# A two-layer decoder step: fewer VectorE instructions, a mask constant of another form, the samples stored with the last quarter, and side products at other places of the matmul stream

## The chip, the cores and the metric

The kernel runs on one core of one Trainium2 chip. The metric is the device time of one execution in microseconds. Three executions of the kernel before took 597.88, 597.41 and 596.48 us, a median of 597.41.

The engines are named as in the profile: PE is TensorE (matrix products, and transposes by a product with the identity), DVE is VectorE, ACT is ScalarE, POOL is GpSimd, and SP is SyncE, which here mostly issues transfers. Each engine works through its own list of instructions in order. An instruction waits on semaphores that other engines or transfers raise.

## The reference, cut to what matters

One step of a decoder with two layers, for a prompt of 256 positions and eight samples of one position each, with 256 earlier positions in a paged cache. All arithmetic is float32.

```python
# layer 0
h = rmsnorm(x, norm_g);  z = h @ w_in                    # q, k, v, bu, bv
a = moba_attention(rope(q), rope(k), v)                  # softmax, causal
bvn = layer_norm(gelu(bv), sgu_gain)
b_out = gelu(bu) * (tril(sgu_w) @ bvn + sgu_b)           # chunks of 128
x = x + concat(a, b_out) @ w_out
x = conv_ffn(x)                                          # x + (gelu(conv3(h @ w_gate)) * (h @ w_up)) @ w_down
# layer 1
q, k, v, u = split(rmsnorm(x) @ w_in)
c = stick_breaking_attention(q, k, v)
pooled = mean of the last w rows of u, w = 2, 4, 8, 16 by group of 128 channels; at position i < w the mean is over i + 1 rows
d = ((pooled - u) @ pool_w) * pool_scale
x = x + concat(c, d) @ w_out
x = conv_ffn(x)
y = rmsnorm(x, final_norm)                               # y_prompt, y_sample
```

The outputs are y for the prompt and the samples, the new keys and values of both layers, the normalised bv rows of the samples, and the new pooling and convolution states.

## The kernel before

**Layout.** Activations lie transposed: 128 channels on the partitions, 264 columns (256 prompt positions, then 8 samples). X holds the residual as eight such slices. Attention probabilities are the other way round, with queries on the partitions, so they are transposed on PE before they meet the values.

**Matrix products.** Each weight block of 128 x 128 is split into a rounded part `wh` (ACT, line 299) and the rest `wl` (DVE, line 302), and each activation likewise into `_h` and `_l`. One block then is three matmuls of 264 columns: wh with h, wh with l, wl with h. A weight tile has eight blocks, and its split is written three tiles ahead of its use (`split`, LOOK = 3). The function `run` goes through a phase's blocks in a fixed order, in0, out0, ff0, dn0, in1, out1, ff1, dn1, with 160, 64, 352, 176, 128, 64, 352 and 176 blocks; `evac` moves a finished accumulator out of PSUM.

**Side work at block numbers.** Everything beside these products is hooked on a block count: `blk(b, f)` calls f once b blocks of the phase are written. Within in0 (bv, q, k, bu, v, 32 blocks each) these are for each pair of heads the scores (`s_qk`) with the softmax behind them (`s_soft`), the transposes of one head's probabilities (`s_tr`), the mean and the squares of the gated branch (`gm_mean`, `gm_var`, `gm_norm`; PE products pmu and ns_sgu), its transposes (`gm_tr`, vtp_sgu) and the gating products (`gm_gate`, pf), the sample scores (`sm_score`, `sm_soft`) and the transposes of the values (`v_pair`, vtp_v). Within in1 (u, q, k, v) they are the pooling sums (`pool_sum`), one pooling product per group (`pool_mix`, pm), the stick-breaking scores (`z_qk`, `stick`), their transposes (`z_tr`, pt), the sample scores (`zs_score`) and again `v_pair`.

**What sets the order.** `keep_in_program_order` fixes the transfers, PE from in0 on, and some single instructions. The others on DVE, ACT and POOL are put in order by a scheduler when the program is built, so that an edit can exchange neighbours on those engines. Accumulators and side products on PE share PSUM banks in rotation: four for the tag mm, four for the tag at.

**Places the change touches.**
- Constants: ones, epst and onesr (lines 385 to 390), made on DVE; the causal mask m0 among the loaded constants, copied twice into mask0 by `masks` (line 760); `sgu_load` (lines 880 to 885) builds a lower triangle tril of zeros and ones out of m0 and the identity on DVE and multiplies the gating weights by it on POOL.
- `zs_score` puts the sample queries into qz (line 474) and `zs_out` the sample results into osam (line 1119) with DVE copies.
- `pool_sum` (line 1139 on) makes, for each of four windows, a doubled sum, the scaled difference pl, and two small instructions hd and pl (lines 1143 and 1144) that correct the first w positions, where the mean is over fewer rows.
- `final` (from line 626): X, scaled by the gain, is transposed back in sixteen pieces `turn(b, m)` into four PSUM banks yt, while row sums of squares give R for the two prompt halves (ns_row) and Rs for the samples (ns_col). DVE and ACT scale the banks into Y, and five stores go out, three on SP and two on ACT.

Of the kernel before, what the change touches and what calls it, by code (L numbers as in the profile page):

```python
# [9 lines left out]
F32 = mybir.dt.float32  # L10
# [8 lines left out]
P = 128  # L19
# [130 lines left out]
def _consts():  # L150
    f = np.float32
    parts = []

    def add(name, a):
        full = np.zeros((P, a.shape[1]), f)
        full[: a.shape[0]] = a
        _CST[name] = (sum(x.shape[1] for x in parts), a.shape[1])
        parts.append(full)

    half = 8  # L160
    inv = (f(500000.0) ** (-(np.arange(half, dtype=f) * f(2.0) / f(16)))).astype(f)
    pos = np.concatenate([np.arange(SEQ), np.full(NS, PAST)]).astype(f)
    ang = (pos[None, :] * inv[:, None]).astype(f)
    c, s = np.cos(ang.astype(np.float64)).astype(f), np.sin(ang.astype(np.float64)).astype(f)
    C, S = np.ones((P, T), f), np.zeros((P, T), f)
    for b in (0, 64):
        C[b:b + 8], C[b + 8:b + 16] = c, c
        S[b:b + 8], S[b + 8:b + 16] = -s, s
    r = np.arange(P)
    global _ROPE, _EDGE  # L170

    _EDGE = np.zeros((P, 384), f)
    _EDGE[r[1:], r[1:]], _EDGE[r, 2 * P + r] = 1, 1
    _ROPE = np.ascontiguousarray(np.concatenate([C, S], 1))
    add("ident", np.eye(P, dtype=f))
    add("m0", np.where(r[None, :] > r[:, None], f(NEG), f(0)).astype(f))
    g32, h32 = r // 32, r % 32
    used = (h32 < 2 * NS)[:, None]
    ts = np.arange(4 * NS)[None, :]
    add("sm", (used & (g32[:, None] == ts // NS) & (h32[:, None] // 2 == ts % NS)).astype(f))  # L180
    add("hs", (used & (h32[:, None] % 2 == r[None, :] // HD)).astype(f))
    add("icnt", np.concatenate([np.tile((f(1) / np.minimum(np.arange(16) + 1, w).astype(f))[None, :], (P, 1)) for w in POOLW], 1))
    return np.ascontiguousarray(np.concatenate(parts, 1))
# [8 lines left out]
    ("sguw", (P, 512)), ("sgub", (P, 512)), ("poolw", (P, 512)),  # L192
]
_OUTS = [
    ("y", (2, P, D)), ("ys", (P, KD, NS)), ("k0", (P, 4, T)), ("v0", (P, 4, T)), ("bvn", (P, 4, NS)),
    ("k1", (P, 4, T)), ("v1", (P, 4, T)), ("poolp", (P, 4, NST)), ("pools", (P, 4, NS, 16)),
    ("cv0", (P, NF, 10)), ("cv1", (P, NF, 10)), ("cs0", (P, NF, NS)), ("cs1", (P, NF, NS)),
]
# [3 lines left out]
def tile_decoder_step(ctx: ExitStack, tc: tile.TileContext, a):  # L202
# [180 lines left out]

    ident = cst("ident")
    ones = con.tile([P, P], F32, name="ones")
    v.memset(ones, 1.0)
    onesr = con.tile([P, P], F32R, name="onesr")
    v.tensor_copy(onesr, ones)
    epst = con.tile([P, 1], F32, name="epst")
    v.memset(epst, EPS)  # L390


    def operand_tile(dst, m, src, gain, pin=False):
# [211 lines left out]
    def final():  # L605
# [25 lines left out]
        def rest():  # L631
            acc = nrm.acc
            p, q = [mmb(f"ns_row{b}") for b in range(2)], mmb("ns_col")
            yt = [[at(f"y{b}{h}") for h in range(2)] for b in range(2)]

            def turn(b, m):
                keep(pe.transpose(yt[b][m // 4][:, m % 4 * P:m % 4 * P + P], X[:, m, b * P:b * P + P], ident))

            def total(b, x, **k):
                keep(pe.matmul(p[b][:, 0:1], x[:, b * P:b * P + P], ones[:, 0:1], **k))  # L640

            R = [sm.tile([P, 1], F32, tag=f"Rf{b}", name=f"R_fin{b}", bufs=1) for b in range(2)]
            Rs = sm.tile([P, NS], F32, tag="Rfs", name="R_fins", bufs=1)

            def rstd(r, x):
                keep(s.activation(r, x, AF.Ln, bias=epst, scale=1.0 / D))
                keep(s.activation(r, r, AF.Exp, scale=-0.5))

            total(0, acc, start=True, stop=False)
            total(1, acc, start=True, stop=False)  # L650
            for m in range(3):
                turn(0, m)
            total(0, sq, start=False, stop=True)
            rstd(R[0], p[0][:, 0:1])
            turn(0, 3)
            total(1, sq, start=False, stop=True)
            rstd(R[1], p[1][:, 0:1])
            for m in range(4, 8):
                turn(0, m)
            keep(pe.matmul(q[:, :NS], ones, acc[:, SEQ:], start=True, stop=False))  # L660
            keep(pe.matmul(q[:, :NS], ones, sq[:, SEQ:], start=False, stop=True))
            for m in range(8):
                turn(1, m)
            Y = [f4(f"y{b}", (P, D)) for b in range(2)]
            ys = sm.tile([P, KD, NS], F32, tag="bvn", name="ys", bufs=1)

            def byv(b, c0, c1):
                keep(v.tensor_scalar(Y[b][:, c0:c1], yt[b][c0 // 512][:, c0 % 512:c0 % 512 + c1 - c0], R[b], None, ALU.mult))

            def bys(b):  # L670
                keep(s.activation(Y[b][:, 512:], yt[b][1], AF.Copy, scale=R[b]))

            def store(e, b, c0, c1):
                keep(e.dma_start(a["y"][b][:, c0:c1], Y[b][:, c0:c1]))

            byv(0, 0, 256)
            store(nc.sync, 0, 0, 256)
            byv(0, 256, 512)
            bys(0)
            store(s, 0, 256, D)  # L680
            rstd(Rs, q[:, :NS])
            byv(1, 0, 512)
            store(nc.sync, 1, 0, 512)
            bys(1)
            keep(v.tensor_tensor(ys, X[:, :, SEQ:T], Rs.unsqueeze(1).to_broadcast([P, KD, NS]), ALU.mult))
            keep(nc.sync.dma_start(a["ys"], ys))
            store(s, 1, 512, D)
        return evac, rest

    def pick(xg):  # L690
# [65 lines left out]
    g.memset(mask0, 0.0)  # L756

    def masks():
        for b in (0, SEQ):
            tc.keep_in_program_order(s.activation(mask0[:, b:b + P], cst("m0"), AF.Copy))  # L760

    q4, k4, v4 = f4("q4"), f4("k4"), f4("v4")
    bv4, bu4 = f4("bv4"), f4("bu4")
# [115 lines left out]
    def sgu_load():  # L879
        late(sguc[:, 0], a["sguw"].rearrange("p (g t) -> p g t", t=P))  # L880
        late(sguc[:, 1], a["sgub"].rearrange("p (g t) -> p g t", t=P))
        tril = sm.tile([P, T], F32, tag="acc", name="tril", bufs=2)[:, :P]
        tc.keep_in_program_order(v.tensor_scalar(tril, cst("m0"), 0.0, None, ALU.is_lt))
        v.tensor_tensor(tril, tril, ident, ALU.add)
        g.tensor_tensor(sguc[:, 0], sguc[:, 0], tril.unsqueeze(1).to_broadcast([P, 4, P]), ALU.mult)

    def sum4(e, t4, name):
        acc = sm.tile([P, T], F32, tag="acc", name=name, bufs=2)
# [82 lines left out]
    blk(64, late, VEC, a["vec"])  # L971
    blk(72, sm_q)
    for t in range(4):
        blk((94, 120)[t // 2], s_qk, t)
    for t, b in enumerate((109, 115, 133, 140)):
        blk(b, s_tr, 2 * t)
        blk(b, s_tr, 2 * t + 1)
    blk(96, sgu_load)
    blk(100, gm_mean)
    blk(119, gm_var)  # L980
    blk(120, sm_score)
    blk(120, sm_soft)
    blk(131, gm_gelu)
    blk(133, gm_norm)
    blk(149, sm_tr)
    blk(120, late, a["k0"], k4)
    blk(156, lambda: late(a["bvn"], st0["bvn"]))
    for t in range(4):
        blk((148, 148, 150, 150)[t], gm_tr, t)
    blk(152, gm_own)  # L990
    for t in range(4):
        blk((153, 153, 157, 157)[t], gm_gate, t)
    for t, b in enumerate((146, 154, 162)):
        if b <= 160:
            blk(b, lambda t=t: v_pair(vt, v4[:, t, :], t, "v0"))
# [106 lines left out]

    def zs_score():
        ps = mmb("sc1")
        sample_score(ps, sample_q(qz1, q4, v.tensor_copy), ktiles, range(NS))
        w = st1["zs"] = pp.tile([P, PAST], F32, tag="p", name="zs")
        stick_all(w, ps[:, :PAST])

# [7 lines left out]
    def zs_out():  # L1116
        osam = sm.tile([P, 4, NS], F32, tag="osam", name="osam1", bufs=1)
        for b, q, po in sample_out(st1["msk"], "l1"):
            v.tensor_copy(osam[b:b + 64, :, q:q + 4], po)
        halves(catA[0][:, :, SEQ:T], catA[1][:, :, SEQ:T], osam)  # L1120


# [10 lines left out]
    def pool_sum():  # L1133
# [3 lines left out]
        for t, W in enumerate(POOLW):  # L1137
            d = A if t % 2 == 0 else B
            v.tensor_tensor(d[:, t:, PW:], src[:, t:, PW:], src[:, t:, PW - W // 2:PW + SEQ - W // 2], ALU.add)
            src = d  # L1140
            v.scalar_tensor_tensor(pl[:, t, :SEQ], src[:, t, PW:], 1.0 / W, U[:, t, PW:], ALU.mult, ALU.subtract)
            hd = sm.tile([P, 16], F32, tag="hd", name=f"hd{t}", bufs=2)
            v.tensor_tensor(hd[:, :W], src[:, t, PW:PW + W], icnt[:, t, :W], ALU.mult)
            v.tensor_tensor(pl[:, t, :W], hd[:, :W], U[:, t, PW:PW + W], ALU.subtract)
            ss = sm.tile([P, NS], F32, tag="ss", name=f"ss{t}", bufs=2)
            v.tensor_reduce(ss, PALL[:, t, :, 16 - W:16], AX.X, ALU.add)
            v.scalar_tensor_tensor(pl[:, t, SEQ:T], ss, 1.0 / W, PALL[:, t, :, NST], ALU.mult, ALU.subtract)

    def pool_mix(t):
        pm = mmb(f"pm{t}")  # L1150
# [29 lines left out]
    blk(84, late, a["poolp"], plp)  # L1180
    blk(84, late, a["pools"], PALL)
    blk(112, late, a["k1"], k4)
    for i, b in enumerate((62, 66, 70, 76)):
        blk(b, pool_mix, i)
    for t, b in enumerate((113, 120, 126)):
        blk(b, lambda t=t: v_pair(vt, v4[:, t, :], t, "v1", mmb))
    run(orders["in1"], pick(xg), in1_evac, hk)
    hk = Hooks()
# [86 lines left out]
```

## Time and profile before

| | us |
|---|---|
| median of three executions | 597.41 |
| the profiled execution | 596.68 |
| its span, first to last instruction | 594.9 |
| PE busy | 586.5 |
| DVE busy | 421.2 |
| ACT busy | 344.5 |
| POOL busy | 108.3 |

The span is what the trace covers; the time of an execution also has what lies around it, here 1.8 us. In a list of instructions a row has the start, the duration, the engine, the line, the operation, what it writes and reads, and in brackets how long the engine was idle before it and what ended that. Matmuls overlap in their pipeline, and one that takes 0.28 us follows the last by 0.12; so PE's throughput is read from the distance of starts, or from the chain of work, which gives a run of matmuls as one piece. The waits list names the waiting instruction, what it waited for, the total in us, how often and the longest. The windows give for a stretch its length, then busy time and number of instructions on each engine, the granted PE clock, the share of the transfer engines' time and GB/s.

### The profile page before, as it was taken

To read this page: it belongs to the slowest core of one execution; us is meant where nothing else is said; L and a number is where in the kernel's file an instruction comes from. 1 tells how busy PE (TensorE), PEld (TensorE's weight loads), DVE (VectorE), ACT (ScalarE), POOL (GpSimd) and SP (SyncE) were. 2 spreads that over 40 slices of the span, in tenths; PEclk is the share of its full clock that TensorE was granted. 3 is DMA by queue.
4 is the path that set the end of the run, shared out by engine and by line. 5 is a ranking of instruction groups with operands and counts; after the bars stand their busy time and mean duration, and the time that the engine had idled before them with its cause. 6 is when DMAs were issued, how large, how long until landed. Compare 5 with 4: busy or idle time off the path is not lost.

```text
span 594.9 us, 12426 instructions
## 1 busy us (share of the span) xinstructions
PE 586.5 (99%) x4913; PEld 571.6 (96%) x4913; DVE 421.2 (71%) x754; ACT 344.5 (58%) x605; POOL 108.3 (18%) x100
## 2 busy tenths in 40 slices
PE   9999999999999999999999999999999999999996
PEld 8998989999999999999999897999999999999995
DVE  6999676878787778665659685687878787864431
ACT  7747955676555555644453475567655555564442
POOL 2100031222322222110110000122232322211110
PEclk9999999999999999999999999999999999999999
DMA  9898872545454555895568765254545555455502
GB/s 342 326 404 310 329 252 82 203 158 197 158 198 166 190 174 182 296 371 188 187 217 290 242 235 177 82 203 156 199 153 202 167 188 175 181 190 196 189 1 74
DMA packets 27708, 122.42 MB, mean 206 GB/s; under 512 B 3458, under 2 KB 4482, under 8 KB 16258
## 3 DMA queue, kind: packets, MB, share of 16 engines
q1 hardware_dynamic: 27072, 120.30, 56.8%
q10 hardware_dynamic: 578, 1.32, 0.6%
q8 instruction: 39, 0.64, 0.4%
q14 instruction: 19, 0.16, 0.1%
HBM read 117.65 MB, written 3.96 MB: 204 GB/s over the span
## 4 chain that ended last, share of the span: by engine, by line
PE 92%; DVE 5%; ACT 1%; issue 1%; DVEq 0%
PE mm L214 84%; DVE wl L302 2%; PE sc L214 1%; PE pv_l L214 1%; PE pav L214 1%; PE pt L217 1%; PE warm L214 1%; DVE keep L1062 1%; PE Z L214 0%; ACT wh L299 0%; PE y L217 0%; DVE rz_k L774 0%; PE pf L214 0%; PE pm L214 0%; PE vtp_v L217 0%
## 5 line engine op out<-in xcount | busy, mean ns | idle before, releaser
L302 DVE TENSOR_TENSOR wl<-raw,wh 128x1024 fp32r<-128x1024 f32 x179 | 218.5, 1222 | 70.0 <-ACT wh L299 64.7
L299 ACT ACTIVATE wh<-raw 128x1024 fp32r<-128x1024 f32 x179 | 188.4, 1055 | 87.5 <-PE mm L214 78.4
L214 PE MATMUL mm<-xg_f_h,wh 128*128 128x264 f32 x704 | 200.1, 284 | 0.0
L214 PE MATMUL mm<-xg_f_l,wh 128*128 128x264 f32 x704 | 199.9, 284 | 0.0
L214 PE MATMUL mm<-xg_f_h,wl 128*128 128x264 f32 x704 | 198.6, 282 | 0.0
L214 PEld LDWEIGHTS mm<-xg_f_l,wh 128*128 128x128 f32 x704 | 132.2, 188 | 0.0
L214 PEld LDWEIGHTS mm<-xg_f_h,wl 128*128 128x128 f32 x704 | 132.2, 188 | 0.0
L214 PEld LDWEIGHTS mm<-xg_f_h,wh 128*128 128x128 f32 x704 | 132.2, 188 | 0.0
L584 POOL TENSOR_TENSOR wk<-wk 128x264 f32<-128x264 f32 x44 | 66.4, 1511 | 193.9 <-DVE wk L583 173.0
L214 PE MATMUL mm<-a_h,wh 128*128 128x264 f32 x352 | 100.1, 284 | 0.0
L214 PE MATMUL mm<-a_l,wh 128*128 128x264 f32 x352 | 99.9, 284 | 0.0
L214 PE MATMUL mm<-a_h,wl 128*128 128x264 f32 x352 | 99.4, 282 | 0.0
L214 PEld LDWEIGHTS mm<-a_l,wh 128*128 128x128 f32 x352 | 66.1, 188 | 0.0
L214 PEld LDWEIGHTS mm<-a_h,wh 128*128 128x128 f32 x352 | 66.1, 188 | 0.0
L214 PEld LDWEIGHTS mm<-a_h,wl 128*128 128x128 f32 x352 | 66.1, 188 | 0.0
L444 ACT ACTIVATE a_h<-wk 128x264 fp32r<-128x264 f32 x44 | 18.7, 424 | 73.1 <-POOL wk L584 73.1
L445 DVE TENSOR_TENSOR a_l<-wk,a_h 128x264 fp32r<-128x264 f32 x44 | 19.2, 436 | 41.5 <-ACT a_h L444 41.5
L214 PE MATMUL mm<-xg_h,wh 128*128 128x264 f32 x160 | 47.5, 297 | 0.0
L214 PE MATMUL mm<-xg_l,wh 128*128 128x264 f32 x160 | 45.8, 287 | 0.0
L214 PE MATMUL mm<-xg_h,wl 128*128 128x264 f32 x160 | 45.6, 285 | 0.0
L214 PE MATMUL mm<-xg_n_h,wh 128*128 128x264 f32 x128 | 38.0, 297 | 0.0
L214 PE MATMUL mm<-xg_n_l,wh 128*128 128x264 f32 x128 | 36.3, 283 | 0.0
(260 smaller groups left out, 903.3 us busy)
## 6 DMA issues: line engine op xcount, KB each, us to landing
raw<-in_w SPq DMA_DIRECT2D x89, 1024.0 KB, 4.8
K<-in_kt SPq DMA_DIRECT2D x32, 256.0 KB, 6.8
V<-in_vp SPq DMA_DIRECT2D x32, 256.0 KB, 5.8
raw<-in_w SPq DMA_DIRECT2D x4, 512.0 KB, 5.8
X<-in_x SPq DMA_DIRECT2D x4, 264.0 KB, 6.4
xw<-in_xw SPq DMA_DIRECT2D x2, 388.0 KB, 5.4
out_k<-k SPq DMA_DIRECT2D x1, 528.0 KB
out_v<-v SPq DMA_DIRECT2D x1, 528.0 KB, 2.8
```

What stands on the lines that cost most here:

```text
L214: return self.keep(nc.tensor.matmul(*x, **k))
L217: return self.keep(nc.tensor.transpose(*x, **k))
L299: i = s.activation(h, src, AF.Copy)
L302: i = v.tensor_tensor(l, src, h.bitcast(F32), ALU.subtract)
L444: s.activation(h, src, AF.Copy)
L445: v.tensor_tensor(l, src, h.bitcast(F32), ALU.subtract)
L584: g.tensor_tensor(A, A, C, ALU.mult)
L1062: v.tensor_tensor_scan(keep[:, 1:n][:, ::-1], keep[:, 1:n][:, ::-1], edge[:, 1:][:, ::-1], 0.0, ALU.mult, ALU.max)
```

## The change

- ones and epst are set by POOL, and onesr is copied by ACT inside `masks`, instead of by DVE.
- The constant m0 (0 and -1e30) becomes low (1 where the column is not below the row, else 0). mask0 is low shifted by one column and scaled by -1e30, and the gating weights are multiplied by low directly; both tril instructions go.
- The copies into qz and osam of layer 1 move from DVE to ACT.
- The eight edge instructions of `pool_sum` become four, each for the two groups whose sums share a buffer, behind all four sums.
- The final stage: four of the second half's transposes come ahead of ns_col. The stores are regrouped into three outputs: y0 in two stores, y1 in one, all three on SP, and y2, the last quarter of the prompt together with the samples, in one store on ACT. ys is no longer a store of its own.
- Block numbers: `s_qk` and `sm_score`, `sm_soft` from 120 to 121, `s_tr` of heads 2 and 3 from 115 to 119, `gm_var` from 119 to 120, `gm_tr` from 148, 148, 150, 150 to 149, 150, 151, 152, the first two `gm_gate` from 153 to 154; in layer 1 `pool_mix` from 62, 66, 70, 76 to 68, 71, 74, 78 and `v_pair` from 113, 120, 126 to 113, 123, 127.

In the built program DVE has 733 instructions in place of 748, ACT 601 in place of 595, POOL 107 in place of 105; PE and SP have as many as before.

```diff
-    add("m0", np.where(r[None, :] > r[:, None], f(NEG), f(0)).astype(f))
+    add("low", (r[None, :] >= r[:, None]).astype(f))
...
-    v.memset(ones, 1.0)
+    g.memset(ones, 1.0)
     onesr = con.tile([P, P], F32R, name="onesr")
-    v.tensor_copy(onesr, ones)
     epst = con.tile([P, 1], F32, name="epst")
-    v.memset(epst, EPS)
+    g.memset(epst, EPS)
...
+            for m in range(4):
+                turn(1, m)
             keep(pe.matmul(q[:, :NS], ones, acc[:, SEQ:], start=True, stop=False))
             keep(pe.matmul(q[:, :NS], ones, sq[:, SEQ:], start=False, stop=True))
-            for m in range(8):
+            for m in range(4, 8):
                 turn(1, m)
...
-            byv(0, 0, 256)
-            store(nc.sync, 0, 0, 256)
-            byv(0, 256, 512)
-            bys(0)
-            store(s, 0, 256, D)
-            rstd(Rs, q[:, :NS])
-            byv(1, 0, 512)
-            store(nc.sync, 1, 0, 512)
-            bys(1)
-            keep(v.tensor_tensor(ys, X[:, :, SEQ:T], Rs.unsqueeze(1).to_broadcast([P, KD, NS]), ALU.mult))
-            keep(nc.sync.dma_start(a["ys"], ys))
-            store(s, 1, 512, D)
+            byv(Y[0][:, :256], 0, 0, 256)
+            keep(nc.sync.dma_start(a["y0"][:, :256], Y[0][:, :256]))
+            byv(Y[0][:, 256:H], 0, 256, H)
+            bys(Y[0][:, H:], 0)
+            keep(nc.sync.dma_start(a["y0"][:, 256:], Y[0][:, 256:]))
+            byv(Y[1], 1, 0, H)
+            keep(nc.sync.dma_start(a["y1"], Y[1]))
             rstd(Rs, q[:, :NS])
+            bys(Y[2][:, :H], 1)
+            keep(v.tensor_tensor(Y[2][:, H:].rearrange("p (m s) -> p m s", s=NS), X[:, :, SEQ:T], Rs.unsqueeze(1).to_broadcast([P, KD, NS]), ALU.mult))
+            keep(s.dma_start(a["y2"], Y[2]))
...
     def masks():
+        tc.keep_in_program_order(s.activation(onesr, ones, AF.Copy))
         for b in (0, SEQ):
-            tc.keep_in_program_order(s.activation(mask0[:, b:b + P], cst("m0"), AF.Copy))
+            tc.keep_in_program_order(s.activation(mask0[:, b + 1:b + P], cst("low")[:, :P - 1], AF.Copy, scale=NEG))
...
-        tril = sm.tile([P, T], F32, tag="acc", name="tril", bufs=2)[:, :P]
-        tc.keep_in_program_order(v.tensor_scalar(tril, cst("m0"), 0.0, None, ALU.is_lt))
-        v.tensor_tensor(tril, tril, ident, ALU.add)
-        g.tensor_tensor(sguc[:, 0], sguc[:, 0], tril.unsqueeze(1).to_broadcast([P, 4, P]), ALU.mult)
+        g.tensor_tensor(sguc[:, 0], sguc[:, 0], cst("low").unsqueeze(1).to_broadcast([P, 4, P]), ALU.mult)
...
-        blk((94, 120)[t // 2], s_qk, t)
-    for t, b in enumerate((109, 115, 133, 140)):
+        blk((94, 121)[t // 2], s_qk, t)
+    for t, b in enumerate((109, 119, 133, 140)):
...
-    blk(119, gm_var)
-    blk(120, sm_score)
-    blk(120, sm_soft)
+    blk(120, gm_var)
+    blk(121, sm_score)
+    blk(121, sm_soft)
...
-        blk((148, 148, 150, 150)[t], gm_tr, t)
+        blk((149, 150, 151, 152)[t], gm_tr, t)
...
-        blk((153, 153, 157, 157)[t], gm_gate, t)
+        blk((154, 154, 157, 157)[t], gm_gate, t)
...
-        sample_score(ps, sample_q(qz1, q4, v.tensor_copy), ktiles, range(NS))
+        sample_score(ps, sample_q(qz1, q4, lambda o, i: s.activation(o, i, AF.Copy)), ktiles, range(NS))
...
-            v.tensor_copy(osam[b:b + 64, :, q:q + 4], po)
+            s.activation(osam[b:b + 64, :, q:q + 4], po, AF.Copy)
...
-            hd = sm.tile([P, 16], F32, tag="hd", name=f"hd{t}", bufs=2)
-            v.tensor_tensor(hd[:, :W], src[:, t, PW:PW + W], icnt[:, t, :W], ALU.mult)
-            v.tensor_tensor(pl[:, t, :W], hd[:, :W], U[:, t, PW:PW + W], ALU.subtract)
...
+        for e, src in enumerate((A, B)):
+            hd = sm.tile([P, 2, 16], F32, tag="hd", name=f"hd{e}", bufs=2)
+            v.tensor_tensor(hd, src[:, e::2, PW:PW + 16], icnt[:, e::2, :], ALU.mult)
+            v.tensor_tensor(pl[:, e::2, :16], hd, U[:, e::2, PW:PW + 16], ALU.subtract)
...
-    for i, b in enumerate((62, 66, 70, 76)):
+    for i, b in enumerate((68, 71, 74, 78)):
         blk(b, pool_mix, i)
-    for t, b in enumerate((113, 120, 126)):
+    for t, b in enumerate((113, 123, 127)):
```

More of the change, by code (lines that the diff above doesn't have):

```diff
@@ L194 @@
 _OUTS = [
-    ("y", (2, P, D)), ("ys", (P, KD, NS)), ("k0", (P, 4, T)), ("v0", (P, 4, T)), ("bvn", (P, 4, NS)),
+    ("y0", (P, D)), ("y1", (P, D // 2)), ("y2", (P, D // 2 + KD * NS)), ("k0", (P, 4, T)), ("v0", (P, 4, T)), ("bvn", (P, 4, NS)),
     ("k1", (P, 4, T)), ("v1", (P, 4, T)), ("poolp", (P, 4, NST)), ("pools", (P, 4, NS, 16)),
@@ L659, in rest, with byv, bys @@
                 turn(0, m)
+            for m in range(4):
+                turn(1, m)
             keep(pe.matmul(q[:, :NS], ones, acc[:, SEQ:], start=True, stop=False))
             keep(pe.matmul(q[:, :NS], ones, sq[:, SEQ:], start=False, stop=True))
-            for m in range(8):
+            for m in range(4, 8):
                 turn(1, m)
[L664 to L674, printed above, removed]
-            byv(0, 0, 256)
-            store(nc.sync, 0, 0, 256)
-            byv(0, 256, 512)
-            bys(0)
-            store(s, 0, 256, D)
-            rstd(Rs, q[:, :NS])
-            byv(1, 0, 512)
-            store(nc.sync, 1, 0, 512)
-            bys(1)
-            keep(v.tensor_tensor(ys, X[:, :, SEQ:T], Rs.unsqueeze(1).to_broadcast([P, KD, NS]), ALU.mult))
-            keep(nc.sync.dma_start(a["ys"], ys))
-            store(s, 1, 512, D)
+            H = D // 2
+            Y = [f4(f"y{i}", (P, w)) for i, w in enumerate((D, H, H + KD * NS))]
+            def byv(dst, b, c0, c1):
+                keep(v.tensor_scalar(dst, yt[b][c0 // H][:, c0 % H:c0 % H + c1 - c0], R[b], None, ALU.mult))
+            def bys(dst, b):
+                keep(s.activation(dst, yt[b][1], AF.Copy, scale=R[b]))
+            byv(Y[0][:, :256], 0, 0, 256)
[5 more added lines that the diff above has]
+            keep(nc.sync.dma_start(a["y1"], Y[1]))
+            rstd(Rs, q[:, :NS])
+            bys(Y[2][:, :H], 1)
+            keep(v.tensor_tensor(Y[2][:, H:].rearrange("p (m s) -> p m s", s=NS), X[:, :, SEQ:T], Rs.unsqueeze(1).to_broadcast([P, KD, NS]), ALU.mult))
+            keep(s.dma_start(a["y2"], Y[2]))
         return evac, rest
@@ L1254 @@
     o = {n: np.asarray(r.results[0]["out_" + n]) for n, _ in _OUTS}
-    y = np.concatenate([o["y"].reshape(SEQ, D), o["ys"].transpose(2, 1, 0).reshape(NS, D)])
+    y1 = np.concatenate([o["y1"], o["y2"][:, :D // 2]], 1)
+    y = np.concatenate([o["y0"], y1, o["y2"][:, D // 2:].reshape(P, KD, NS).transpose(2, 1, 0).reshape(NS, D)])
     def kv(k, w):
```

## The prediction

> **What bounds the kernel now.** I read the page's first part, then the list of what TensorE (PE) waited for, then the busy time by stage.
>
> ```profile
> span 594.9 us, 12426 instructions
> ...
> PE 586.5 (99%) x4913; PEld 571.6 (96%) x4913; DVE 421.2 (71%) x754; ACT 344.5 (58%) x605; POOL 108.3 (18%) x100
> ```
>
> ```profile
> PE pt L217 <- DVE p L811: 1.0, 1, 1.0
> PE vtp_v L217 <- DVE v4b L1164: 0.6, 1, 0.6
> ```
>
> ```profile
> 18.73:52.35 33.62, 32.59 (x272) 31.78 (x270) 32.95 (x91) 22.99 (x43) 1.29 (x1) 1.00 0.94 363
> ...
> 350.00:375.00 25.00, 24.45 (x217) 20.65 (x217) 14.69 (x22) 15.29 (x32) 0.00 (x0) 1.00 0.53 170
> ...
> 400.18:586.50 186.32, 186.32 (x1541) 186.32 (x1541) 122.22 (x202) 101.82 (x167) 40.84 (x28) 1.00 0.46 160
> 586.50:594.90 8.40, 2.86 (x25) 2.39 (x24) 2.38 (x8) 2.98 (x10) 0.00 (x0) 0.94 0.36 130
> ```
>
> The columns are PE, PEld, DVE, ACT and POOL, then the granted clock and the DMA share. PE has no gap in the long stages and the change takes no matmul away, so only three things can get shorter: the two PE waits, each inside a stage where DVE's queue runs late (32.95 of 33.62 us busy in the first), and the last 8.4 us, where PE is nearly done and copies and stores end the kernel. A DVE instruction saved anywhere else is worth nothing.
>
> **The first wait (layer 0).** PE's own rows:
>
> ```profile
> 50.83 0.49 PE L217 MATMUL pt<-CST,p 128*128 128x128 f32 x3
> 52.35 0.55 PE L217 MATMUL pt<-CST,p 128*128 128x128 f32 x3 [1.03 <-DVE p L811]
> ```
>
> ```profile
> 52.90 1.47 PE mm L214 x12
> 54.36 0.45 PE pmu L214 x2
> ```
>
> Three transposes at 0.11 us each from 50.83 would have let the next start at 51.16; it started at 52.35, so 1.19 us is lost. The change puts these transposes (heads 2 and 3) behind block 119 instead of 115: four blocks of three matmuls, 12 x 0.122 = 1.47 us. PE then asks for the fourth head's probabilities at about 50.83 + 1.47 + 0.33 = 52.63. What is ready by then:
>
> ```profile
> 46.73 0.22 DVE L883 TENSOR_SCALAR tril<-CST 128x128 f32<-128x128 f32 x1
> ...
> 48.95 0.29 DVE L884 TENSOR_TENSOR tril<-tril,CST 128x128 f32<-128x128 f32 x1
> ...
> 49.58 1.38 DVE L890 TENSOR_TENSOR bsum<-bsum,bv 128x264 f32<-128x264 f32 x1
> ...
> 52.02 0.27 DVE L811 TENSOR_SCALAR p<-p,st 128x128 f32<-128x128 f32 x1
> 52.22 0.42 DVE L891 TENSOR_TENSOR bsum<-bsum,bv 128x264 f32<-128x264 f32 x1
> ```
>
> ```profile
> 49.38 1.29 POOL L885 TENSOR_TENSOR sguc<-sguc,tril 128x512 f32<-128x512 f32 x1 [32.78 <-DVE tril L884]
> ```
>
> The DVE normalisation ended at 52.29, so even unchanged it is ready 0.3 us ahead of PE. The two tril instructions leave the queue: from start to start they take 0.14 and 0.21 us. The second bsum addition took 1.38 us where the third took 0.42: the 0.96 us lies under the POOL multiply of 1.29 us, which now waits only for its weights, no longer for tril. Its start is bounded by 49.38 (now) and, were its transfer landed long before, by DVE's earlier two-input operations; the collision costs DVE between 0 and 1.29 us. I take the measured 0.96, so DVE is 0.35 us ahead and the margin is 0.7 us; at 1.29 it is still 0.3. The Trainium skill, "SBUF — State Buffer", section "Who interferes with whom", has DVE instructions with two SBUF inputs locked out for a whole POOL instruction that reads SBUF. By that rule the loss would be up to the full 1.29 us, and the end of the sum is the same; the trace agrees on the block (1.38 against 0.42).
>
> Head scores and their mean matmul (pmu) shift from 119/120 to 120/121, in the same order, and bsum's third addition (52.64 at the latest) is there before PE reaches pmu at about 53.3. So this wait goes whole: 1.19 us, bounds 0.9 and 1.2.
>
> **What is late next in layer 0.** ACT does not get earlier: in the new order a weight copy stands ahead of mu on ACT, the matching weight difference ahead of the subtraction on DVE, and the last head's Copy behind a table load, so its row of work up to the layer norm's scale keeps its hours. PE arrives there 1.19 us sooner.
>
> ```profile
> 70.69 0.44 ACT L434 ACTIVATE R_sgu<-R_sgu 128x264 f32<-128x264 f32 x1
> ```
>
> ```profile
> 71.96 1.70 DVE L917 SCALAR_TENSOR_TENSOR bv<-bv,VEC,R_sgu 128x264 f32<-128x264 f32 x4
> ```
>
> ```profile
> 72.67 0.27 PE vtp_sgu L217 x2
> ...
> 73.77 0.22 PE pP L217 x2
> 73.99 0.14 PE pO L214 x2
> ```
>
> Before, PE met the first vtp_sgu at 72.67. Now block 148 comes at 71.48, then a block (0.37) and pP and pO (0.36): 72.2. The first of four normalised slices is ready a quarter into 1.70 us, at 72.4. PE waits 0.2 us, and the spread over blocks 149 to 152 lets the other three pass; before, the pair at 148 lost about as much (pitch 0.25 between slices one and two). I count 0; bounds -0.2 and +0.6. The gating products stand one block later and find their slices ready.
>
> **The second wait (layer 1).**
>
> ```profile
> 357.83 0.28 PE L214 MATMUL mm<-xg_n_h,wl 128*128 128x264 f32 x1
> 358.66 0.44 PE L217 MATMUL vtp_v<-CST,v4b 128*128 128x128 f32 x2 [0.55 <-DVE v4b L1164]
> ```
>
> ```profile
> 358.20 0.41 DVE L1164 TENSOR_TENSOR v4b<-mm,R_n 128x264 f32<-128x264 f32 x1
> ...
> 360.12 0.42 DVE L1164 TENSOR_TENSOR v4b<-mm,R_n 128x264 f32<-128x264 f32 x1
> ```
>
> PE could have gone on at 357.95; 0.71 us is lost on v4b, held up by stick-breaking on DVE. Moved from 120 to 123, the transpose comes after three blocks (1.1) and six score transposes (0.66, their weights long done): 359.7, and v4b is there at 358.61. The next one, at 127, comes at 359.7 + 0.22 + 1.47 = 361.4, and its slice at 360.54. Gain 0.71, bounds 0.4 and 0.75.
>
> **Pooling and moved copies.**
>
> ```profile
> 326.42 0.41 DVE L1141 SCALAR_TENSOR_TENSOR pl<-poolb,poolu 128x256 f32<-128x256 f32 x1
> ...
> 328.05 0.17 DVE L1144 TENSOR_TENSOR pl<-hd,poolu 128x16 f32<-128x16 f32 x1
> ```
>
> ```profile
> 326.31 0.45 PE pm L214 x2
> ```
>
> ```profile
> L489 ACT ACTIVATE PZ<-pP 128x32 f32<-128x32 f32 x8 | 0.9, 208 | 0.2 <-PE pP L217 0.2
> ```
>
> ```profile
> 375.18 0.73 DVE L1119 COPY osam<-po_l 64x16 f32<-64x16 f32 x4 [1.24 <-PE po_l L217]
> ```
>
> Eight edge operations become four, but now all groups wait for the last two. DVE's order puts the final pieces right behind the fourth scaled sum and one q: about 327.2. The first pm moves from block 62 to 68, 326.31 + 2.2 = 328.5: margin 1.3 us, nothing gained, nothing lost. Without the margin it would cost PE one for one. The four osam copies take 0.73 us on DVE; on ACT, idle then, copies of that size take 0.21 each, at most 0.84 together, and their reader is on ACT too, which saves the handover: 0, with a loss of 0.1 as the bound. PE has four blocks of other products between the transposes and the first use. The two qz copies end long before the sample scores. Constants made on POOL, and onesr on ACT, have their first use tens of microseconds later: 0.
>
> **The end.**
>
> ```profile
> 588.09 0.35 PE ns_col L214 x4
> 588.43 0.83 PE y L217 x7
> ...
> 589.27 0.28 ACT R_fins L646
> ...
> 589.57 0.21 ACT R_fins L647
> ```
>
> ```profile
> 590.38 0.35 ACTq L674 DMA_DIRECT2D out_y<-y  x1
> 590.56 0.46 SPq L686 DMA_DIRECT2D out_ys<-ys  x1
> ```
>
> ```profile
> out_y<-y ACTq DMA_DIRECT2D x1, 256.0 KB, 3.1
> ...
> out_ys<-ys SPq DMA_DIRECT2D x1, 32.0 KB, 3.1
> ```
>
> ys is issued last, 590.56, and lands 3.1 us later. The change takes ACT's first store away (SP issues it and has nothing behind it until DVE's last slice), so R_fins follows ns_col at about 588.95 instead of 589.27, and the last copy starts when PE's transposes end, 589.39, not after R_fins. It ends about 0.3 us sooner, 590.06, and one store with the samples goes out at 590.09, 0.47 us ahead of the old last issue. Landing 3.1 to 3.2 us: gain 0.45, bounds 0 and 0.5. The Trainium skill, "DMA: Bandwidth & Descriptors", "Specifications", has transfers under 512 B read, modify and write; ys has 256 B a partition. By that rule its removal would gain beyond the issue; here both landed in 3.1 us, so I add nothing.
>
> **Sum.** 1.19 + 0 + 0.71 + 0.45 = 2.35 us. The profiled execution took 596.68 us, 0.73 under the median of the three; it would become 594.3. On the median: 597.41 - 2.35 = 595.1 us.
>
> **Rivals.**
> - The wait is passed on. ACT's row of work is what limits layer 0's end, and PE stands at vtp_sgu or pf for all the 1.19 us. For it: ACT's unmoved times. Against: 0.2 us in my count. Gain 1.16, time 596.25.
> - The two PE waits go but the end does not: the combined store lands later, or DVE's last multiply is late. Gain 1.9, time 595.5. For it: 288 KB instead of 256 in the last store; against: equal landing times at 32 and 256 KB.
> - Slower: the pooled pieces come too late for the first pm. That decides once they are over 1.3 us later than counted; to end 0.2% slower they must be 1.3 + 2.35 + 1.2 = 4.9 us late, time 598.6. Against: DVE has fewer operations there.
>
> **Chances.** A difference under 0.2% (1.2 us) can't be told from none. Forecast 0.62, wait passed on 0.17 (it lies at the border, so I count it as same), end unchanged 0.13 (faster), late pooling 0.08 (slower). Faster 0.75, same 0.17, slower 0.08. The forecast's own bounds give 594.5 to 596.1; with the runs' spread of 1.4 us and the first rival the range is 593.9 to 597.3.
>
> **What would show it.** Right: no PE idle before pt or vtp_v; a wait of 0 to 0.6 us at vtp_sgu; the last store issued at about 588.2 (590.09 less the two waits), and its landing the end. Wrong: PE idle at pm, pt or vtp_sgu above 0.6 us, or y2 landing more than 3.4 us after its issue.

## The result, and the profile after

The changed kernel takes 594.18 us (median of 7 runs, 593.88 to 594.90) where the kernel before, run beside it, takes 597.06. The ratio is 0.9947, with a 95% interval of 0.9933 to 0.9961: by the ratio 3.2 us faster, 2.3 to 4.0 (the medians differ by 2.9). The forecast was 2.35 us (595.1, a ratio of 0.9961). The direction was right, but the gain is larger than forecast: 594.18 is faster than the forecast's own bounds allow (594.5 to 596.1), and lies near the lower end of the wide range (593.9 to 597.3). The two profiled executions differ by 2.71 us (596.68 and 593.97) against the 2.35 of the sum; their spans differ by 2.65.

The page's first rows after:

```profile
span 592.2 us, 12416 instructions
...
PE 585.9 (99%) x4913; PEld 571.5 (96%) x4913; DVE 419.1 (71%) x739; ACT 344.9 (58%) x612; POOL 107.5 (18%) x102
```

What PE waited for after (in total, times, longest):

```profile
PE warm L214 <- DVE warm L374: 1.2, 1, 1.2
PE vtp_sgu L217 <- DVE bv L912: 0.5, 1, 0.5
```

The wait at warm, at the start, is the same before. Both waits that the prediction looked at are gone, and the one at vtp_sgu that the prediction allowed for (0 to 0.6 us) is there. The timeline at the three places, PE first (start, duration, engine):

```profile
52.12 0.82 PE L217 MATMUL pt<-CST,p 128*128 128x128 f32 x6
...
72.47 0.44 PE L217 MATMUL vtp_sgu<-CST,bv 128*128 128x128 f32 x2 [0.49 <-DVE bv L912]
```

```profile
51.53 0.28 DVE L809 TENSOR_SCALAR p<-p,st 128x128 f32<-128x128 f32 x1
```

```profile
358.72 0.38 PE L217 MATMUL vtp_v<-CST,v4b 128*128 128x128 f32 x2
```

The last probabilities are ready at 51.81 us; PE comes to them after three transposes, at about 52.45. The six transposes now run through without a gap.

The end, in the timeline after:

```profile
587.00 0.63 PE L217 MATMUL y<-CST,X 128*128 128x128 f32 x4
...
587.67 0.69 ACT L672 ACTIVATE y<-y,R_fin 128x512 f32<-128x512 f32 x1
587.71 0.33 SPq L680 DMA_DIRECT2D out_y<-y  x1
587.72 0.23 DVE L683 TENSOR_TENSOR y<-X,R_fins 128x64 f32<-128x64 f32 x1
588.39 0.38 ACTq L684 DMA_DIRECT2D out_y<-y  x1
```

```profile
out_y<-y ACTq DMA_DIRECT2D x1, 288.0 KB, 2.5
out_y<-y SPq DMA_DIRECT2D x1, 256.0 KB, 2.5
```

The same places in the timeline before, PE's last transposes and DVE's last wide multiply:

```profile
588.29 1.07 PE L217 MATMUL y<-CST,X 128*128 128x128 f32 x8
...
589.38 0.75 DVE L668 TENSOR_SCALAR y<-y,R_fin 128x512 f32<-128x512 f32 x1 [0.64 <-PE y L217]
```

A landing is counted from the issue of a store to the completion that the trace shows for it. PE's last transpose ends at 587.63 (before: 589.36). The last store is issued 0.76 us later (before: 590.56, 1.20 later) and lands in 2.52 us; ys took 3.13. From PE's last transpose to the last landing it is 3.28 us after and 4.33 before.

Setting PE's 4416 block matmuls of both traces side by side splits the span's 2.65 us: 0.17 at the start (chance: k3 and k5 below, whose start is that of the kernel before, differ from it there by 0.26 and 0.31); 1.26 at pt, of which 0.42 comes back at vtp_sgu; 0.73 at vtp_v; 1.05 between PE's end and the last landing; and 0.13 lost between the last landing and the last instruction.

### The profile page after: what moved, and what is told of

Same layout as the page of the kernel before. It is cut to its first block, busy times and chain, and to the rows that moved or that the text cites. A ratio compares the mean times of both kernels' runs of the same rounds, so it can differ in the third digit from the quotient of the medians.

```text
span 592.2 us, 12416 instructions
## 1 busy us (share of the span) xinstructions
PE 585.9 (99%) x4913; PEld 571.5 (96%) x4913; DVE 419.1 (71%) x739; ACT 344.9 (58%) x612; POOL 107.5 (18%) x102
## 3 DMA queue, kind: packets, MB, share of 16 engines
HBM read 117.65 MB, written 3.96 MB: 205 GB/s over the span
## 4 chain that ended last, share of the span: by engine, by line
PE 96%; ACT 3%; issue 1%; DVE 0%
PE mm L214 89%; PE pv_l L214 1%; PE pav L214 1%; PE warm L214 1%; PE pt L217 1%; PE sc L214 1%; ACT p L807 1%; PE Z L214 1%; ACT wh L299 0%; PE pf L214 0%; PE pm L214 0%; ACT pT L820 0%; PE vtp_v L217 0%; PE S L214 0%; PE y L217 0%
## 5 line engine op out<-in xcount | busy, mean ns | idle before, releaser
L302 DVE TENSOR_TENSOR wl<-raw,wh 128x1024 fp32r<-128x1024 f32 x179 | 218.9, 1225 | 72.2 <-ACT wh L299 69.3
```

The costliest lines, as they stand in the source:

```text
L302: i = v.tensor_tensor(l, src, h.bitcast(F32), ALU.subtract)
```

## Experiments

The question is the end: 1.05 us where 0.45 was forecast, and the excess is in the landing, not in the issue. Three theories: only the issue counts, with a fixed landing time (the prediction's); the 256 B per partition of ys land late; or, from the trace of before, a third. In its last stretch this view of the DMA engines (slices of 0.15 us from 588.0; busy tenths, then GB/s) shows a tail, and a packet that belongs to no store:

```profile
DMA  0000000069759998992189999999994000000000
GB/s 0 0 0 0 0 0 0 0 232 369 253 205 369 389 471 348 389 369 82 55 287 416 382 341 342 410 410 369 369 245 101 31 15 19 0 0 0 0 0 0
...
q14 instruction: 1, 0.01, 0.3%
```

The q14 packet is 8 KB of instructions. It starts at 590.93 and holds one DMA engine for 0.31 us. Until about 592.5 some 16 store packets are under way at a time; from 592.64 to 593.11 they come one behind the other. The trace doesn't name the engine of a packet, but this is what one engine looks like that started its share late while the others are done; and a store has landed only when its last packet has. Also, DVE's last 512-wide multiply (L668) begins at 589.38 although the wait just ahead of it ended at 588.99 (the row above puts the idle time down to PE's last transposes, which this multiply doesn't read; in k13 below it starts 0.05 us behind that wait). Counting DVE's instructions in the trace with its waits and branches (the page's x754 leaves these out), that multiply is number 960 of 966, and DVE's earlier q14 packets come about 128 instructions, 8 KB, apart. After the change DVE has 949 in all and never gets to number 960; the page counts 18 q14 packets instead of 19, and none lies among the stores. This is the fetch theory: the engine's program comes in by such packets, and the change made DVE's program so short that it ends ahead of its last one.

**The end alone, and the end put back.** k1_tail_only is the kernel before with the change's end; k2_tail_back is the reverse.

```diff
-            Y = [f4(f"y{b}", (P, D)) for b in range(2)]
+            Y = [f4(f"y{i}", (P, w)) for i, w in enumerate((D, H, H + KD * NS))]
...
-            keep(nc.sync.dma_start(a["ys"], ys))
-            store(s, 1, 512, D)
+            keep(s.dma_start(a["y2"], Y[2]))
```

> The kernel before with the change's end alone (three outputs, samples in the last store, y1's transposes ahead of the sample norm). PE's waits at pt (1.0 us) and vtp_v (0.6 us) stay, PE's last transpose ends at about 589.4 us, the last store is issued at 590.1 instead of 590.56. Issue theory (the prediction's: only the time of the last issue counts, landing 3.1 us): 0.45 us faster. Small-store theory (256 B per partition land late, and that store is gone): landing 2.5 us, 1.05 us faster. Fetch theory (one DMA engine is held by an 8 KB instruction packet of DVE at the end, and DVE's number of instructions is unchanged): the packet is still there, landing 2.8 to 3.1 us, 0.45 to 0.75 us faster.

> The changed kernel with the end of the kernel before put back (two outputs y and ys, five stores). PE ends as in the changed kernel, about 587.6 us. Small-store theory: ys lands 3.1 us after its issue, the time is 1.05 us above the changed kernel, 1.7 us below the kernel before. Fetch theory: DVE has too few instructions for another fetch, so ys lands 2.6 to 2.7 us after its issue; 0.5 to 0.65 us above the changed kernel, 2.1 below the kernel before. Issue theory: 0.45 us above the changed kernel, landing not predicted.

k1: 596.40 us, ratio 0.9994 (0.9985 to 1.0003). The last store is issued at 590.07 as counted, and lands 3.19 us later, although no 256 B store is left. So the small-store theory's 2.5 us is out. A fixed landing of 3.1 us would fit this run alone as well, but the view also shows the packet:

```profile
q14 instruction: 1, 0.01, 0.6%
...
out_y<-y ACTq DMA_DIRECT2D x1, 288.0 KB, 3.2
```

k2: 594.75 us, ratio 0.9962 (0.9949 to 0.9976). No q14 packet, and ys, the same store that took 3.13 us, lands in 1.91; the last to land is the quarter that ACT stores, 2.30 us after its issue and 3.33 after PE's end. So the small-store theory falls from both sides, and a fixed landing time too. And by the traces the new end itself is worth 0.05 us (3.33 against 3.28) once the packet is gone; the medians of k2 and the changed kernel differ by 0.6 us, with intervals that overlap.

**DVE's instruction count alone.** k13_off_path takes from the kernel before only what the prediction priced at nothing; k12_pad gives the changed kernel 15 empty DVE instructions.

```diff
-    v.tensor_copy(onesr, ones)
...
-            v.tensor_copy(osam[b:b + 64, :, q:q + 4], po)
+            s.activation(osam[b:b + 64, :, q:q + 4], po, AF.Copy)
...
-            v.tensor_tensor(hd[:, :W], src[:, t, PW:PW + W], icnt[:, t, :W], ALU.mult)
...
+            v.tensor_tensor(hd, src[:, e::2, PW:PW + 16], icnt[:, e::2, :], ALU.mult)
```

> The kernel before with only those removals from DVE that the prediction priced at nothing (three constants, two qz copies, four osam copies, the pooled pieces two groups at a time with their products six blocks later): 13 DVE instructions fewer. PE's waits at pt (1.0) and vtp_v (0.6) stay and PE ends within 0.1 us of the kernel before; the last store is issued at 590.56. Issue theory and small-store theory: no gain, landing 3.1 us. Fetch theory: DVE ends short of its last fetch boundary, no instruction packet among the last stores, ys lands 2.6 to 2.7 us after its issue, 0.4 to 0.5 us faster.

```diff
+            for _ in range(15):
+                tc.keep_in_program_order(v.memset(junk, 0.0))
```

> The changed kernel with 15 empty DVE instructions (memsets of 128x2) in the middle of the last FFN's first half, where DVE has idle time; nothing else moves. Fetch theory: DVE counts 964 instructions again, passes its last fetch boundary (about 959) within its last five instructions, and an 8 KB instruction packet falls among the last stores, at about 588.6 to 589: the last store lands 2.8 to 3.0 us after its issue instead of 2.5, 0.3 to 0.5 us slower than the changed kernel. Issue and small-store theories: no change, landing 2.5 us, within 0.1 us of the changed kernel.

k13 (953 DVE instructions): PE keeps its two waits and ends within 0.13 us of the kernel before, and the stores of the old end now read

```profile
GB/s 0 0 0 0 0 0 0 20 294 335 219 253 410 430 389 389 348 396 355 396 341 396 309 376 435 396 382 314 28 0 0 0 0 0 0 0 0 0 0 0
...
out_y<-y ACTq DMA_DIRECT2D x1, 256.0 KB, 2.3
out_y<-y SPq DMA_DIRECT2D x1, 128.0 KB, 1.7
out_ys<-ys SPq DMA_DIRECT2D x1, 32.0 KB, 1.9
```

The low tail of the GB/s row is gone. DVE's 512-wide multiply now begins 0.33 us before PE's last transpose ends (at 589.23 here), not 0.02 after, so its store goes out earlier too:

```profile
588.90 0.75 DVE L667 TENSOR_SCALAR y<-y,R_fin 128x512 f32<-128x512 f32 x1 [0.29 <-PE y L217]
```

With both gone, it is 3.33 us from PE's end to the last landing instead of 4.33. The time is 596.56 us, ratio 0.9990 (0.9978 to 1.0003): the interval holds the 1.0 us and also none, so it is the trace that decides here. k12 (964): the packet is back and the landing is 3.21 us, more than the 2.8 to 3.0 expected. Its ratio is 0.9969 (0.9957 to 0.9980), 1.3 us above the changed kernel; the packet explains 0.7 of that, and the profiled execution lost another 1.0 us at 24 us by a late weight transfer (below).

**The wait at vtp_sgu.** k6_sgu_later puts the pairs one or two blocks later; k0_after is the changed kernel once more.

```diff
-        blk((149, 150, 151, 152)[t], gm_tr, t)
+        blk((151, 151, 152, 153)[t], gm_tr, t)
-        blk((154, 154, 157, 157)[t], gm_gate, t)
+        blk((155, 155, 157, 157)[t], gm_gate, t)
```

> The changed kernel with the four vtp_sgu pairs behind blocks 151, 151, 152, 153 instead of 149 to 152, and the first two gating products behind 155 instead of 154. If the 0.42 us that PE lost there was only a matter of place (the normalised slices ready at 72.4 us, PE there at 72.0), the wait of 0.5 us at vtp_sgu goes, PE passes the gating products without a new wait and ends 0.4 us sooner than in the changed kernel; the end stays as it is (last landing 3.3 us after PE's last transpose). If the delay is passed on (gating products or the first out-projection blocks late), PE ends within 0.1 us of the changed kernel.

> The changed kernel itself once more, beside the others on the same chip. PE's waits: none at pt and vtp_v, 0.5 us at vtp_sgu. Fetch theory: no 8 KB instruction packet of DVE near the end, the last store lands 2.4 to 2.6 us after its issue and 3.2 to 3.4 us after PE's last transpose; 2.4 to 3.2 us faster than the kernel before. If the short landing was chance: landing up to 3.2 us.

k6: 593.78 us, ratio 0.9945 (0.9932 to 0.9959); k0: 594.63, 0.9960 (0.9945 to 0.9975). In k6 the wait at vtp_sgu is gone and no new one came; against the changed kernel's trace PE is 0.13 us behind before it and 0.21 ahead after it, a gain of 0.34, and ends at 587.42. This version has the lowest median of the complete kernels, 593.56 to 594.09 us in five runs, though its interval overlaps with the changed kernel's; with the start behind it PE waits for nothing that the waits list shows. k0 has the short landing again (2.53 us, 3.28 after PE's end).

**The packet put back where nothing else waits.** k16_best_pad is k6 with k12's 15 instructions.

> The kernel with the later vtp_sgu pairs, in which PE had no wait left, plus the 15 empty DVE instructions (964 again). Fetch theory: an 8 KB packet of DVE's instructions falls among the last stores, the last store lands 3.1 to 3.3 us after its issue instead of 2.53, 3.9 to 4.0 us after PE's last transpose instead of 3.29; 0.6 to 0.7 us slower than without them, so a ratio to the kernel before of about 0.9955 instead of 0.9945. Rival (the long landings were chance): landing 2.5 us, ratio 0.9945.

594.48 us, ratio 0.9961 (0.9945 to 0.9977), 0.7 us above k6. DMA view of its last stretch:

```profile
GB/s 0 0 0 0 0 0 0 0 0 212 355 266 321 328 369 410 369 389 348 383 396 389 375 374 379 411 427 350 292 46 31 15 31 0 0 0 0 0 0 0
...
q14 instruction: 1, 0.01, 0.7%
...
out_y<-y ACTq DMA_DIRECT2D x1, 288.0 KB, 3.1
```

Landing 3.13 us instead of 2.53, 3.89 us after PE's end instead of 3.29. This time the packet took 0.66 us of one engine (587.94), and in the tail of 46, 31, 15, 31 GB/s the packets again come one behind the other. The intervals of k6 and k16 overlap; the 0.60 us is read from the traces.

**Layer 0 and layer 1 taken apart.** k3_in0_moves: the kernel before with the change's block numbers for head scores, probabilities, `gm_var` and sample scores, while `gm_tr` and `gm_gate` stay at 148, 148, 150, 150 and 153; k4_tril_only: without the tril instructions; k5_in1_move: with layer 1's block numbers.

```diff
-    for t, b in enumerate((109, 115, 133, 140)):
+    for t, b in enumerate((109, 119, 133, 140)):
```

> The kernel before with layer 0's seven block numbers alone (tril stays on DVE). By the prediction's count DVE's last normalisation is ready 0.3 us ahead of PE even so: the wait at pt goes (1.2 us), 0.4 to 0.5 us of it comes back at vtp_sgu, PE ends 0.7 to 0.8 us sooner. DVE has 966 instructions, so the fetch at the end stays (last store lands 4.3 us after PE's last transpose). Rival: the removal of tril is what frees PE, and 0.3 us or more of the wait at pt stays.

```diff
-        tril = sm.tile([P, T], F32, tag="acc", name="tril", bufs=2)[:, :P]
-        tc.keep_in_program_order(v.tensor_scalar(tril, cst("m0"), 0.0, None, ALU.is_lt))
-        v.tensor_tensor(tril, tril, ident, ALU.add)
```

> The kernel before without the two tril instructions on DVE (mask constant instead), block numbers unchanged. DVE saves 0.35 us, so the wait at pt shrinks from 1.0 to 0.65 us; if the 0.96 us collision with the POOL product goes as well, the wait vanishes. vtp_v's wait of 0.6 stays. DVE has 964 instructions: the fetch at the end stays.

```diff
-    for t, b in enumerate((113, 120, 126)):
+    for t, b in enumerate((113, 123, 127)):
```

> The kernel before with layer 1's three block numbers alone (the second and third vtp_v pair behind 123 and 127). The wait at vtp_v (0.6 to 0.7 us) goes with no new one, PE ends 0.7 us sooner; pt's wait stays, and DVE's fetch at the end (966 instructions) too.

k3: 597.45 us, ratio 1.0005 (0.9995 to 1.0014). Over ten runs nothing is gained. The wait at pt is no longer listed, but 1.2 us comes back at vtp_sgu:

```profile
PE vtp_sgu L217 <- DVE bv L917: 1.2, 1, 1.2
PE vtp_v L217 <- DVE v4b L1164: 0.6, 1, 0.6
PE mm L214 <- DVE bv L782: 0.5, 1, 0.5
```

```profile
71.83 0.45 ACT L434 ACTIVATE R_sgu<-R_sgu 128x264 f32<-128x264 f32 x1
72.73 1.70 DVE L917 SCALAR_TENSOR_TENSOR bv<-bv,VEC,R_sgu 128x264 f32<-128x264 f32 x4
```

DVE and ACT had been 0.8 us late since 24 us in this execution (the third wait above), and PE, which had caught up, met them again. That is the first rival's mechanism: the slices come behind ACT's row, whose weight copy stood at 69.37 us before and at 69.35 in the changed kernel, although PE was 1.4 us ahead there. It cost more here than in the changed kernel for two reasons that k3 doesn't part: the transposes were left at block 148, and the start was disturbed.

k4 (596.96, one run beside 597.01): the wait at pt is 1.2 us, no shorter. The POOL multiply starts sooner and hits another DVE instruction, the first addition of bsum:

```profile
48.51 1.53 DVE L886 TENSOR_TENSOR bsum<-bv 128x264 f32<-128x264 f32 x1
```

k5 (596.00, one run): the wait at vtp_v goes, PE gains 0.7 us there, nothing follows. Its end has the packet, and is as long as before (4.34 us).

**Pooled products, and the queue of stores.**

```diff
-    for i, b in enumerate((68, 71, 74, 78)):
+    for i, b in enumerate((62, 66, 70, 76)):
```

> The changed kernel with the pooled products back behind blocks 62, 66, 70 and 76 (the pooled pieces still two groups at a time). In the changed kernel the last piece ends at 326.6 us and PE would come to block 62 at 325.1 us: PE waits 1.4 to 1.5 us at pm, and ends that much later. If the pieces were no later than before: no wait.

```diff
-            keep(nc.sync.dma_start(a["y0"][:, 256:], Y[0][:, 256:]))
```

> The changed kernel without the second store of the end (384 KB of y0 stay unwritten, which is left out on purpose). If the last store's landing of 2.5 us is mostly the queue of bytes issued before it (1.06 MB from the first store's issue on, moved at about 355 KB per us), it lands 2.0 us after its issue, 0.5 us sooner; if each store needs 2.5 us by itself, nothing moves.

k8 (595.57, one run): PE waits 0.7 us at pm (L1143 releases it) and is 0.9 us later behind the four products than ahead of them. Less than expected: the last piece ended at 326.7, as counted, but PE, late since the start in this execution, came to pm at 325.9 instead of 325.1. So the later blocks are needed once the pieces come two groups at a time. k10 (593.88, one run): the last store lands 2.15 us after its issue instead of 2.52; 0.37 of the 0.5 expected. Without a packet in the way, part of a landing is the queue of bytes ahead of it.

The end of all kernels, from PE's last transpose to the last landing (k10, with a store less, is left out):

| kernel | DVE instructions, waits included | q14 packet among the stores | us |
|---|---|---|---|
| before, k5 (old end) | 966, 966 | yes | 4.33, 4.34 |
| k3, k4 (old end) | 965, 964 | yes | 4.18, 4.18 |
| k13, k2 (old end) | 953, 949 | no | 3.33, 3.33 |
| k1, k12, k16 (new end) | 966, 964, 964 | yes | 3.95, 3.96, 3.89 |
| after, k0, k6, k8 (new end) | 949 | no | 3.28, 3.28, 3.29, 3.29 |

## Where the prediction was wrong, and where it was right

The step that failed is the end. The prediction took a landing of 3.1 to 3.2 us as fixed and counted the earlier issue alone: 0.45 us, bounds 0 and 0.5. The end gave 1.05, because the last landing fell to 2.52 us: the changed DVE program stops short of the 8 KB instruction packet that had fallen among the last stores. A second term was put at nothing and measured 0.42 us lost (vtp_sgu). Term by term:

- **First wait, 1.19 us: right.** 1.26 us measured. Also right that DVE would have been in time even unchanged: in k3, with tril in place, DVE was 0.87 us late there and PE 0.48, and PE lost about 0.1 us, the counted margin of 0.3 less those 0.39.
- **DVE 0.35 + 0.96 us earlier without tril: wrong in its second part.** The collision did not go, it moved. In the changed kernel the POOL multiply starts at 48.27 and hits the two own products:

```profile
48.27 1.30 POOL L880 TENSOR_TENSOR sguc<-sguc,CST 128x512 f32<-128x512 f32 x1 [31.62 <-DVE bsum L884]
```

```profile
48.17 1.45 DVE L839 TENSOR_TENSOR own<-q,k 64x32 f32<-64x32 f32 x2
```

  Before, those two took 0.38 together. The normalisation came 0.49 us sooner, 0.17 of it from the start. Nothing hung on it: the margin was 0.64 us where 0.7 was counted. The rule cited there from the Trainium skill, "SBUF — State Buffer", section "Who interferes with whom", fits these three places (1.38 us here before, 1.26 for the second own product, 1.53 in k4, beside POOL's 1.3 to 1.5); an earlier POOL multiply only chose another victim. In k12 the multiply met the normalisation of another head, which took 1.41 us where it takes 0.28 elsewhere. That one reads one matrix and a column of scalars; whether the rule takes in such an instruction no run here shows.
- **What is late next, 0: mis-sized, 0.42 us lost.** It lies inside the bounds (-0.2 to +0.6). PE was at vtp_sgu at 71.98, earlier than the 72.2 counted; the slice came at 72.4 as counted. The 72.2 was reckoned from 72.67, where the chain's piece begins; in the timeline before, the first of these products starts at 72.50. From there the same count gives 72.0 and a wait of 0.4. So a third of the first gain was passed on, the first rival's mechanism, and k6 shows that one or two blocks more would have avoided it.
- **Second wait, 0.71 us: right.** 0.73 in the changed kernel, 0.7 alone in k5.
- **Pooling and copies, 0: right on PE, with a smaller margin.** The last piece ended at 326.58 and pm began at 327.30: 0.7 us, not 1.3. k8 shows the wait that the old block numbers would bring. The rival of late pooling did not come.
- **The end, 0.45 us: the failed step.** "Landing 3.1 to 3.2 us" was taken over as a property of the stores. The last issue moved 0.44 us nearer to PE's end as worked out, but that was worth 0.05 us when no packet was in the way (k2 against the changed kernel) and 0.38 when one was (k1). The gain of 1.05 came from DVE's shorter program: 1.0 us at the old end (k13), 0.6 to 0.7 at the new (k12, k16).
- **"A DVE instruction saved anywhere else is worth nothing": wrong.** k13 saves only such instructions, and its end is 1.0 us shorter. It is their number that counts here, not their time.
- The sum against the spans: 1.19 + 0 + 0.71 + 0.45 = 2.35 was forecast; 1.26 - 0.42 + 0.73 + 1.05 = 2.62 came, with 0.17 from the start and 0.13 lost in the barrier. Two errors of opposite sign, 0.42 and 0.60, partly covered each other: that the sum came as near as it did is luck. The remaining distance to the measured 3.2 us lies within the interval.
- The forecast's own bounds, 594.5 to 596.1, don't follow from the bounds of its terms. These add up to a gain of 0.6 to 2.65 us (0.9 - 0.6 + 0.4 - 0.1 + 0, and 1.2 + 0.2 + 0.75 + 0.5), which is 594.8 to 596.8.

## What to carry to other kernels

When a kernel ends in stores, look at the last microseconds of its DMA packets and not only at issue and landing: a low tail in the GB/s row says that some engine is late, and a packet that belongs to no store can say why. An instruction removed off the path can pay, and one added can cost, when the engine's program ends just past such a refill; a few empty instructions in an idle stretch test it. When a stall is removed by doing other work first, the next consumer of the same late engine needs the same shift, or it takes part of the gain back, or, as in k3, all of it.

## What the runs showed of the hardware that was not expected

- DVE's program comes in 8 KB packets about 128 instructions apart. Where the last wide multiply was number 960, six instructions ahead of the end (before, k1, k5), DVE also paused 0.3 to 0.4 us at it, with nothing to wait for that the trace shows; where number 960 came behind that multiply (k3, k4, k12, k16), no pause is seen and only the packet costs. What causes the pause was not tested. The Trainium skill, "Runtime: NRT & Kernel Launch", section "Instruction fetch mechanics", has each engine's sequencer refill its own instruction store in blocks while it executes, at a cost that is mostly hidden; at the end of this kernel it was not hidden: it cost 0.6 to 1.0 us. What the earlier packets cost was not tested.
- The packet itself takes 0.31 to 0.67 us, and the last landing comes 0.6 us or more later. At the new end (k1, k12, k16) the packet's time (0.57 to 0.67) and the delay (0.6 to 0.7) are alike. In k3 and k4, without the pause, it is recorded with 0.31 us, yet the last packets come one at a time for 0.8 us, and the landing is 0.85 later; why more is lost there than the packet's own time is open.
- The start is where executions of one kernel differ. In k12 a 1 MB weight transfer issued at 10.2 us landed at 20.0; in the changed kernel one issued at 10.3 landed at 17.3. In k12 DVE fell behind by about 1 us, and PE waited at 24 us:

```profile
PE mm L214 <- DVE bv L787: 0.8, 1, 0.8
```

  PE lost 0.2 to 1.0 us there in the six traces where that transfer landed at 18.9 us or later (k10, k4, k8, k0, k3, k12), and nothing in the eight where it landed by 18.4. It is as large as the terms of this prediction, so terms of this size are read from traces aligned block by block.
